# A recurrence stage whose interleaving is re-weighted: priorities for five streams, a tile-aware model, 64x64 tiles and a triangular inverse in one piece

## The chip, the core and the metric

The kernel runs on one core of a Trainium2 chip. The metric is the device time of one execution in microseconds (us). The engines are TensorE (PE), VectorE (DVE), ScalarE (ACT), GpSimd (POOL) and SyncE (SP, which issues most DMAs).

## The reference

One sequence of 512 tokens of width 1024 passes through an attention layer with an MLP, a recurrent layer with an MLP, and a second block with two further recurrences. All edits of code but those of the cost model are in the recurrent layer, RWKV-7, that runs in both directions over 16 heads of 64:

```python
xs = tuple(jnp.moveaxis(t, 1, 0) for t in (r, w, k, v, kk, a))
_, out = lax.scan(step, jnp.zeros((nB, H, N, N), F32), xs)
...
r = mix(0) @ w_r
k = mix(2) @ w_k
v = mix(3) @ w_v
...
for d in range(2):
    ...
    decay = jnp.exp(-jnp.exp(w_log.astype(F32)))
    a = jax.nn.sigmoid(a0[d] + (xa @ a1[d]) @ a2[d])
    g = jax.nn.sigmoid(xg @ g1[d]) @ g2[d]
    kd = heads(k * (1 + (a - 1) * k_a))
    ...
    o = rwkv7_scan(*ins)
    ...
    bonus = jnp.sum(rh * kd * r_k.astype(F32), axis=-1, keepdims=True) * vh
    dir_out.append((group_norm(o, gn_w, gn_b) + bonus.reshape(nB, S, D)) * g.astype(F32))
y = dir_out[0] + dir_out[1]
return y.astype(h.dtype) @ w_o
```

The step of the scan updates, for each head and direction, a 64x64 state that decays, forgets along `kk` and takes in `v` along `kd`; the output is the state read along `r`.

## The kernel before

**How the scan is tiled.** The scan is computed in chunks of 64 tokens, eight for each direction. Two heads make a pair p, and the pairs p = 0 to 7 follow one another. For each pair the work is cut into generator functions, the streams, in `rwkv` (from L1507):

- `values` (L1507): the projection `v`, with weights split into two parts (matmuls `mb<-mx,whi` and `mb<-mx,wlo`); it runs once over all columns.
- `front` and `half` for each direction d: the low-rank decays and gates (`mb<-lhl,wh`), a running sum on DVE, exponentials on ACT, and 16 products into tiles `ar` and `bk`, 128x256 each.
- `scores` (four iterations i): the chunk's products (`mb<-ar,bk`), two masks on DVE into `at`, stores of the diagonal blocks to DRAM (`nd`), transposes of `bk` (`mb<-ident,bk`).
- `inverse` (L1694): reads the diagonal blocks back into `X` and `XL` and inverts 128 unit triangles of 16x16 on DVE, by 28 small products and sums, then stores `X` to DRAM.
- `early`: loads `v`, spreads it over the tiles `uv` (`mb<-cmat,v`).
- `merge`: loads the inverses (`yd`), transposes them (`zd`) and builds the inverse of 64x64 from the small ones, by some 200 matmuls on 32x32 tiles of PE with copies between.
- `mid` (four iterations i, two chunks each): `ahead` (`mb<-ident,ar`, `mb<-uv,at`), `ax`, the product with the inverse (`mb<-ax,tt`), `ta`, and `mb<-at,ta`, whose result with `ar` and the identity becomes the transition `m`.
- `chain`: eight steps. Each one multiplies the state `ss` with `m` (`cp<-ss,m`), adds what the chunk brings (`cp<-uv,at`), and copies and scales the new state by four ACT copies, and the output `o` by two.
- `post`: the norm of the heads (two squares on ACT, two reduces into `rg` on DVE, a power on POOL, two multiplies `o<-o,rg` on DVE), transposes (`mb<-ident,o`), the bonus and the gate.

**What orders the work.** `Net.weave` (L36) takes the streams and interleaves them by a model: it asks each stream for its next piece, computes from `cost` (L48) and `wait` when that piece could start, and emits the one that starts first, less the stream's lead. On each engine the instructions then run in exactly the order of their emission, since `account` ties each to the one before it. Three stages are built this way: the attention, the scan, and the second block. A stream may also yield a condition: `chain(p)` waits until `post(p-1)` is done; `scores` are held at most nine tiles of `at` ahead of the chain; `mid` at most three transitions `m`; `early` starts with the chain of p-1; `inverse` waits for the four scores, `merge` for `inverse` and `early`. PSUM has five banks with the tag `mb` for all but the chain, which has three of its own.

For PE, `cost` tells tiles side by side apart by their column alone.

Of the kernel before, what the change touches and what calls it, by code (L numbers as in the profile page):

```python
# [10 lines left out]
F32 = mybir.dt.float32  # L11
# [13 lines left out]
class Net:  # L25
# [10 lines left out]
    def weave(self, streams, slow=1.0):  # L36
# [5 lines left out]
        seen = len(nc.cur_bb.bb.instructions)  # L42
        free, ready, last, used, cols, table = {}, {}, {}, [128], {}, [AF.Exp]

# [3 lines left out]
        def cost(i, e, t):  # L48
            n = math.prod(c for _, c in i.outs[0].ap[1:])
            if e == "PE":  # L50
                (_, col), (rows, m) = i.tile_position, i.tile_size
                if m == 128 or m != used[0] or col in used[1:]:
                    used[:] = [m]
                beside = len(used) > 1
                used.append(col)
                one = i.ins[0].dtype in (F32R, mybir.dt.bfloat16)
                passes = 2 if i.is_transpose else 1 if one else 4

                tick = int(t / 3.413)
                c = passes * (max(n, 64) if one or i.is_transpose else m / 2 if beside else max(n, m)) * 0.417e-3  # L60
                c *= slow if cols.get(tick - 1, 0) > 3060 else 2 * slow
                tick = int((t + c) / 3.413)
                cols[tick] = cols.get(tick, 0) + passes * n * rows / 128
                return c + 0.004
# [1226 lines left out]
    def rwkv(self, g_pre, mu_p, mu_n, w_r, w_k, w_v, w_o, k_k, k_a, r_k, gn_w, gn_b, w0, w1, w2, a0, a1, a2,  # L1291
# [35 lines left out]
        with ExitStack() as c0:  # L1327
# [110 lines left out]
            with ExitStack() as c1:  # L1438
# [4 lines left out]
                self.weights(cw, 2, 2)  # L1443
                vout = self.pool(cw, "vout")
                late = {}
# [11 lines left out]

                tts, ss, tas = zeros("tt", [8, 2, 64]), zeros("ss", [2, 128]), zeros("ta", [2, 2, 2, 64])
                for j, t in enumerate(tts + ss + tas):
                    (V, G)[j % 2].memset(t, 0.0)  # L1460
# [46 lines left out]
                def values():  # L1507
# [14 lines left out]
                    for j in range(KD):  # L1522
# [7 lines left out]
                        yield AC, b  # L1530
                        t = vout.tile([128, S], F32, name="vo", tag="vo")
                        ACT(t, b, AF.Copy)
# [161 lines left out]
                def inverse(p, st):  # L1694

                    yield lambda: done["pre"] > p
                    XL = sh.tile([128, 16, 32], F32, name="XL", tag="v1")
                    for q in range(2):
# [8 lines left out]
                    for j in range(1, 15):  # L1707
                        n = 15 - j
                        t = xt[:, :j * n].rearrange("p (i c) -> p i c", c=n)
                        TT(V, t, X[:, 0:j, j].unsqueeze(2).to_broadcast([128, j, n]),  # L1710
                           X[:, j, j + 1:16].unsqueeze(1).to_broadcast([128, j, n]), M)
                        yield DV, xt
                        TT(V, X[:, 0:j, j + 1:16], X[:, 0:j, j + 1:16], t, AD)
                        yield DV, X
                    V.memset(flat(X)[:, 0:512:33], 1.0)
# [3 lines left out]
                def early(p, st):  # L1719
# [7 lines left out]
                    st["uv"] = uv  # L1727
                    for d in range(2):
                        yield PO,
                        G.memset(uv[d][H(d)], 0.0)  # L1730
                    yield PE, v
# [79 lines left out]
                def mid(p, st):  # L1811
# [5 lines left out]
                    def ahead(i):  # L1817
                        b = bank().rearrange("p (j h e x) -> p j h e x", j=2, h=2, e=2)
                        at = st["q", i]
                        for j in range(2):  # L1820
# [3 lines left out]
                            for hp in range(2):  # L1824
                                for d in range(2):
                                    MM(b[H(d), j, hp, 1, :], at[:, j, hp, 2 * d, H(d)], uv[d][:, cs[d], hp, :], True, True)
                        return b

                    for i in range(4):
# [17 lines left out]
                        yield AC, b  # L1847
                        ta = tas[i % 2]
                        for d in range(2):
                            ACT(ta[H(d), d], b[H(d), :, :, 0:64], AF.Copy)  # L1850
                        yield AC, b
# [3 lines left out]
                        yield PE, ta  # L1855
                        b = bank().rearrange("p (j d x) -> p j d x", j=2, d=2)
                        for j in range(2):
                            for d in range(2):
                                for hp in range(2):
                                    MM(b[H(hp), j, d, :], ta[:, d, j, hp, :], lhs(at[:, j], d, hp), True, True)  # L1860
                        yield DV, b
                        m = mp.tile([128, 2, 2, 128], F32, name="m", tag="m", bufs=3)
                        for d in range(2):
                            cs = slice(6 - 2 * i, 8 - 2 * i) if d else slice(2 * i, 2 * i + 2)
                            r = ar[d][:, cs, 1 - d, :]
                            TT(V, m[:, :, d, H(d)], b[:, :, d, H(d)], r[:, ::-1] if d else r, AD)
                        i4 = lambda t: t.rearrange("p j d x -> p j (d x)")[:, :, 64:192].rearrange("p j (d x) -> p j d x", d=2)
                        TT(V, i4(m), i4(b), ident2.unsqueeze(1).unsqueeze(1).to_broadcast([128, 2, 2, 64]), AD)
                        st["m", i] = m
# [94 lines left out]
                def each(f):  # L1964
                    for p in range(8):
                        yield from f(p, sts[p])

                self.weave([(values(), 0.0)] + [(each(f), 0.0) for f in (
                    chain, mid, inverse, early, merge, scores, front, lambda p, st: half(p, st, 0), lambda p, st: half(p, st, 1), post)])


# [166 lines left out]
```

## Time and profile before

| | |
|---|---|
| median of 3 runs | 2333.58 us (2332.74 to 2334.99) |
| the profiled execution | 2329.99 us |
| its span | 2328.2 us |
| mean granted clock of TensorE | 0.952 |
| busy over the span: PE, DVE, ACT, POOL | 2135.0, 1276.4, 1077.6, 85.3 us |

The profiled execution is 3.6 us below the median. Busy time tells how long an engine had an instruction under way. A matmul in 32-bit floats shows as two records, so the counts of the trace are twice those of the code. The clock granted to PE is a share of 2.4 GHz.

### The profile page before, as it was taken

The page shows a single profiled execution, that of the slowest core. Times are in us where ns is not written, and L with a number is a line of the kernel's source. Part 1 is how long each engine was busy: PE and PEld are TensorE (multiplying, and loading weights), DVE is VectorE, ACT ScalarE, POOL GpSimd, SP SyncE. Part 2 cuts the span into 40 slices and gives each one's busy share as a digit, 9 for nine tenths or more (in the row PEclk, how much of TensorE's full clock was granted, in tenths as well). Part 3 has the DMA queues.
Part 4 walks back from the last instruction along what each step waited for, and adds up shares of the span by engine and source line. Part 5 has one row for each costly group of instructions (what it writes and reads, how often), then busy time and mean ns, then how long its engine had stood idle before and what let it go on. Part 6 is the DMA issues. An engine that isn't in the chain of part 4 may idle for free. (4 is left out here: it accounts for less than half of the span.)

```text
span 2328.2 us, 40334 instructions
## 1 busy us (share of the span) xinstructions
PE 2135.0 (92%) x16330; PEld 1719.8 (74%) x16330; DVE 1276.4 (55%) x2562; ACT 1077.6 (46%) x1950; POOL 85.3 (4%) x123
## 2 busy tenths in 40 slices
PE   7898999999968788888898689999999999999998
PEld 6777788888856666666676568887787877788877
DVE  4656542333388765667664255387645566633353
ACT  4555353342356554777766544333233444522232
POOL 0000000000000000011100100000000000000000
PEclk9999999999979987989999899999999988899999
DMA  5311233233224233222222343324334544233341
GB/s 173 104 55 54 71 110 92 90 100 100 91 71 121 91 99 80 61 61 57 52 55 46 105 133 109 91 90 144 111 111 142 143 126 119 54 95 90 107 145 55
DMA packets 321028, 221.52 MB, mean 95 GB/s; under 512 B 82414, under 2 KB 274442, under 8 KB 320842
## 3 DMA queue, kind: packets, MB, share of 16 engines
q1 hardware_dynamic: 319402, 213.70, 32.3%
q10 hardware_dynamic: 1440, 5.24, 0.7%
q8 instruction: 129, 2.11, 0.4%
q14 instruction: 57, 0.47, 0.1%
HBM read 187.62 MB, written 27.07 MB: 92 GB/s over the span
## 5 line engine op out<-in xcount | busy, mean ns | idle before, releaser
L160 ACT ACTIVATE whi<-raw 128x1024 fp32r<-128x1024 f32 x220 | 231.1, 1052 | 585.9 <-PE mm L223 297.3
L161 DVE TENSOR_TENSOR wlo<-raw,whi 128x1024 fp32r<-128x1024 f32 x220 | 266.5, 1214 | 368.0 <-ACT whi L160 365.4
L222 PE MATMUL mm<-uth,whi 128*128 128x512 f32 (+1 forms) x1088 | 412.9, 382 | 2.1 <-ACT uth L196 2.1
L223 PE MATMUL mm<-utl,whi 128*128 128x512 f32 (+1 forms) x1088 | 406.6, 374 | 5.5 <-DVE utl L197 5.5
L224 PE MATMUL mm<-uth,wlo 128*128 128x512 f32 (+1 forms) x1088 | 406.6, 374 | 0.0
L223 PEld LDWEIGHTS mm<-utl,whi 128*128 128x128 f32 x1088 | 209.0, 192 | 43.2 <-DVE utl L197 6.7
L222 PEld LDWEIGHTS mm<-uth,whi 128*128 128x128 f32 x1088 | 208.3, 192 | 41.0 <-ACT uth L196 3.5
L224 PEld LDWEIGHTS mm<-uth,wlo 128*128 128x128 f32 x1088 | 208.8, 192 | 37.3 <-issue 1.1
L224 PE MATMUL mm<-whi,hl 128*128 128x512 f32 x512 | 200.6, 394 | 0.0
L222 PE MATMUL mm<-whi,hh 128*128 128x512 f32 x512 | 200.5, 394 | 0.0
L223 PE MATMUL mm<-wlo,hh 128*128 128x512 f32 x512 | 199.9, 393 | 0.0
L224 PEld LDWEIGHTS mm<-whi,hl 128*128 128x128 f32 x512 | 96.3, 188 | 22.0 <-issue 0.2
L223 PEld LDWEIGHTS mm<-wlo,hh 128*128 128x128 f32 x512 | 96.3, 188 | 21.6
L222 PEld LDWEIGHTS mm<-whi,hh 128*128 128x128 f32 x512 | 96.3, 188 | 21.5 <-issue 0.4
L222 PE MATMUL mm<-whi,uth 128*128 128x512 f32 x224 | 88.6, 401 | 8.5 <-ACT whi L160 6.4
L224 PE MATMUL mm<-whi,utl 128*128 128x512 f32 x224 | 88.7, 399 | 0.0
L223 PE MATMUL mm<-wlo,uth 128*128 128x512 f32 x224 | 88.5, 398 | 0.0
L1301 ACT ACTIVATE ss<-cp,wc 64x64 f32<-64x64 f32 x224 | 69.1, 309 | 27.6 <-PE cp L1302 22.7
L282 DVE TENSOR_TENSOR acc<-mm,acc 128x512 f32<-128x512 f32 x48 | 33.0, 688 | 77.6 <-PE mm L224 77.6
L223 PE MATMUL mm<-mx,whi 128*128 128x512 f32 x160 | 66.0, 412 | 4.6 <-DVE mx L1289 4.4
L222 PE MATMUL mm<-mx,whi 128*128 128x512 f32 x160 | 62.1, 415 | 7.2 <-ACT mx L1288 6.0
L1299 DVE SCALAR_TENSOR_TENSOR mt<-u_pad,vcol,mt 128x512 f32<-128x512 f32 x96 | 66.8, 745 | 1.4 <-ACT mt L1301 1.3
(554 smaller groups left out, 3966.3 us busy)
## 6 DMA issues: line engine op xcount, KB each, us to landing
raw<-in_mlp_w_dram SPq DMA_DIRECT2D x128, 512.0 KB
raw<-in_w_in_dram SPq DMA_DIRECT2D x44, 512.0 KB
raw<-in_attn_w_in_dram SPq DMA_DIRECT2D x18, 512.0 KB
gbt<-in_norm_g_dram ACTq DMA_DIRECT2D x8, 512.0 KB
raw<-in_attn_w_out_dram SPq DMA_DIRECT2D x8, 512.0 KB
raw<-in_rk_w_k_dram SPq DMA_DIRECT2D x8, 512.0 KB
h_s<-h SPq DMA_DIRECT2D x8, 512.0 KB
raw<-in_rk_w_r_dram SPq DMA_DIRECT2D x8, 512.0 KB
```

The lines of the kernel that those rows point to most:

```text
L160: nc.scalar.activation(out=hi[:, :n], in_=raw[:, :n], func=AF.Copy)
L161: nc.vector.tensor_tensor(out=lo[:, :n], in0=raw[:, :n], in1=hi[:, :n].bitcast(F32), op=ALU.subtract)
L222: mm(out, lhsT=lhs[0], rhs=rhs[0], start=start, stop=False)
L223: mm(out, lhsT=lhs[0], rhs=rhs[1], start=False, stop=False)
L224: mm(out, lhsT=lhs[1], rhs=rhs[0], start=False, stop=stop)
L282: nc.vector.tensor_tensor(out=a, in0=p, in1=a, op=ALU.add)
L1299: STT = lambda e, o, a, s, b, o0, o1: e.scalar_tensor_tensor(out=o, in0=a, scalar=s, in1=b, op0=o0, op1=o1)
L1301: ACT = lambda o, i, f, **k: nc.scalar.activation(out=o, in_=i, func=f, **k)
```

## The change

The change has nine parts, all in one diff: (1) `cost` knows a tile by its rows, columns and place, and counts a small fixed time for a tile beside another one; (2) the pool `vout` goes, `values` use the buffers of `TQ()`; (3) the zeroed tiles `tas` go, `ta` is written by one ACT copy of 128x256 in place of two of 64x256; (4) `XL` has a buffer of its own; (5) `inverse` doesn't yield between its 28 products; (6) `early` doesn't zero halves of `uv`; (7) `ahead` multiplies 64 rows of `at` and `uv`; (8) `mid` multiplies `at` and `ta` by halves, on four 64x64 tiles, into two banks, and `m` is made by four sums of 128x128; (9) `chain` has a lead of 0.5, `mid`, `merge` and `inverse` of 0.4, `early` of 0.3.

```diff
         def cost(i, e, t):
             n = math.prod(c for _, c in i.outs[0].ap[1:])
             if e == "PE":
-                (_, col), (rows, m) = i.tile_position, i.tile_size
-                if m == 128 or m != used[0] or col in used[1:]:
-                    used[:] = [m]
+                at, (rows, m) = i.tile_position, i.tile_size
+                if (rows, m) != used[0] or at in used[1:]:
+                    used[:] = [(rows, m)]
                 beside = len(used) > 1
-                used.append(col)
+                used.append(at)
...
-                c = passes * (max(n, 64) if one or i.is_transpose else m / 2 if beside else max(n, m)) * 0.417e-3
+                c = passes * (max(n, 64) if one or i.is_transpose else 8 if beside else max(n, 64)) * 0.417e-3
...
-                        t = vout.tile([128, S], F32, name="vo", tag="vo")
+                        t = TQ()
...
-                    XL = sh.tile([128, 16, 32], F32, name="XL", tag="v1")
+                    XL = sh.tile([128, 16, 32], F32, name="XL", tag="XL")
...
                            X[:, j, j + 1:16].unsqueeze(1).to_broadcast([128, j, n]), M)
-                        yield DV, xt
                         TT(V, X[:, 0:j, j + 1:16], X[:, 0:j, j + 1:16], t, AD)
-                        yield DV, X
...
-                    for d in range(2):
-                        yield PO,
-                        G.memset(uv[d][H(d)], 0.0)
...
-                                    MM(b[H(d), j, hp, 1, :], at[:, j, hp, 2 * d, H(d)], uv[d][:, cs[d], hp, :], True, True)
+                                    MM(b[H(d), j, hp, 1, :], at[H(1 - d), j, hp, 2 * d, H(d)], uv[d][H(1 - d), cs[d], hp, :], True, True)
...
-                        ta = tas[i % 2]
-                        for d in range(2):
-                            ACT(ta[H(d), d], b[H(d), :, :, 0:64], AF.Copy)
+                        ta = mp.tile([128, 2, 2, 64], F32, name="ta", tag="ta")
+                        ACT(ta, b[:, :, :, 0:64], AF.Copy)
...
-                        b = bank().rearrange("p (j d x) -> p j d x", j=2, d=2)
+
+                        bs = [bank()[:, :256].rearrange("p (j x) -> p j x", j=2) for _ in range(2)]
                         for j in range(2):
-                            for d in range(2):
-                                for hp in range(2):
-                                    MM(b[H(hp), j, d, :], ta[:, d, j, hp, :], lhs(at[:, j], d, hp), True, True)
-                        yield DV, b
+                            for hp in range(2):
+                                for d in range(2):
+                                    MM(bs[d][H(hp), j, :], ta[H(d), j, hp, :], lhs(at[:, j], d, hp)[H(d)], True, True)
                         m = mp.tile([128, 2, 2, 128], F32, name="m", tag="m", bufs=3)
                         for d in range(2):
+                            yield DV, bs[d]
...
-                            TT(V, m[:, :, d, H(d)], b[:, :, d, H(d)], r[:, ::-1] if d else r, AD)
-                        i4 = lambda t: t.rearrange("p j d x -> p j (d x)")[:, :, 64:192].rearrange("p j (d x) -> p j d x", d=2)
-                        TT(V, i4(m), i4(b), ident2.unsqueeze(1).unsqueeze(1).to_broadcast([128, 2, 2, 64]), AD)
+                            TT(V, m[:, :, d, H(d)], bs[d][:, :, H(d)], r[:, ::-1] if d else r, AD)
+                            TT(V, m[:, :, d, H(1 - d)], bs[d][:, :, H(1 - d)], ident2.unsqueeze(1).to_broadcast([128, 2, 64]), AD)
...
-                self.weave([(values(), 0.0)] + [(each(f), 0.0) for f in (
+                lead = {chain: 0.5, mid: 0.4, merge: 0.4, inverse: 0.4, early: 0.3}
+                self.weave([(values(), 0.0)] + [(each(f), lead.get(f, 0.0)) for f in (
                     chain, mid, inverse, early, merge, scores, front, lambda p, st: half(p, st, 0), lambda p, st: half(p, st, 1), post)])
```

**How the order moves.** Three places, a row as the engine's order has it.

PE at the end of `values`, before: the last products of `values` (`mx,...`) are followed by the first stage of `merge(0)` (`zd,at` and `yd,at`).

```order
L222 MATMUL mb<-mx,whi 128x512
L223 MATMUL mb<-mx,whi 128x512
L224 MATMUL mb<-mx,wlo 128x512
L1302 MATMUL mb<-zd,at 32x32 x2
L1302 MATMUL mb<-yd,at 32x32 x2
```

And with the change: they are followed by `ahead(0)` of `mid(0)`.

```order
L222 MATMUL mb<-mx,whi 128x512
L223 MATMUL mb<-mx,whi 128x512
L224 MATMUL mb<-mx,wlo 128x512
L1302 MATMUL mb<-ident,ar_6222 64x2x64
L1302 MATMUL mb<-ident,ar_6227 64x2x64
L1302 MATMUL mb<-uv_6672,at 64x64
```

`merge(0)` now stands between earlier products of `values`.

DVE in `post(2)`, before: the first multiply `o<-o,rg` with what stands around it; `xt` and `X` are the inverse.

```order
L1298 TENSOR_TENSOR xt__9981<-X 128x44
L1298 TENSOR_TENSOR X<-X,xt__9981 128x4x11
L1298 TENSOR_TENSOR xt__9981<-X 128x50
L1298 TENSOR_TENSOR X<-X,xt__9981 128x5x10
L1298 TENSOR_TENSOR xt__9981<-X 128x54
L1298 TENSOR_TENSOR X<-X,xt__9981 128x6x9
L1298 TENSOR_TENSOR xt__9981<-X 128x56
L1298 TENSOR_TENSOR X<-X,xt__9981 128x7x8
L1298 TENSOR_TENSOR o<-o,rg 128x512
L1300 TENSOR_SCALAR rn<-mb 128x8
L1298 TENSOR_TENSOR xt__9981<-X 128x56
L1300 TENSOR_SCALAR tmp<-tmp 128x8x64
```

And with the change: the end of the inverse, which now lies whole between the power and the first multiply, then both multiplies; `tmp<-r,tmp` and `wl` are of `half` and `front`.

```order
L1298 TENSOR_TENSOR xt__10054<-X 128x26
L1298 TENSOR_TENSOR X<-X,xt__10054 128x13x2
L1298 TENSOR_TENSOR xt__10054<-X 128x14
L1298 TENSOR_TENSOR X<-X,xt__10054 128x14
L1712 MEMSET X 128x16
L1298 TENSOR_TENSOR tmp<-r,tmp 128x512
L1298 TENSOR_TENSOR wl<-w,wh 128x512
L1298 TENSOR_TENSOR o<-o,rg 128x512
L1298 TENSOR_TENSOR at<-mb,mk 128x2x2x128 x2
L1654 COPY bns<-mb 128x8 x2
L1299 SCALAR_TENSOR_TENSOR tmp<-mb,vcol_4919,tmp 128x256 x2
L1298 TENSOR_TENSOR o<-o,rg 128x512
```

From `post`'s first reduce to its second multiply there are now 73 instructions, and 34 before; the 16 products of `half` are among them.

PE in `chain(3)`, before: twelve rows between two of its steps (`cp<-...`), of `mid`, of `scores` (`ar,bk`, `ident,bk`).

```order
L1302 MATMUL mb<-ax,tt_6032 64x128 x8
L1302 MATMUL mb<-ar_9800,bk_9803 128x128 x2
L1302 MATMUL mb<-ar_9808,bk_9809 128x128 x2
L1302 MATMUL mb<-ar_9800,bk_9803 128x128 x2
L1302 MATMUL mb<-ar_9808,bk_9809 128x128 x2
L1302 MATMUL mb<-at,ta_6035 64x128 x8
L1687 MATMUL mb<-ident,bk_9803 128x128
L1687 MATMUL mb<-ident,bk_9809 128x128
L1687 MATMUL mb<-ident,bk_9803 128x128
L1687 MATMUL mb<-ident,bk_9809 128x128
L1302 LDWEIGHTS zb
L1302 MATMUL cp<-zb 128x256
```

And with the change: twelve rows after the fourth step. One product of `mid` and one of `post` (`lg`) lie between, and the scores stand behind the last steps or in the gap between two chains.

```order
L1302 MATMUL cp<-ss_6031,m 128x128 x2
L1302 MATMUL mb<-ax,tt_6029 64x128 x8
L1302 MATMUL mb<-lg_4941,wg 128x512
L1302 LDWEIGHTS zb
L1302 MATMUL cp<-zb 128x256
L1302 MATMUL cp<-uv_9199,at 64x64 x4
L1302 MATMUL cp<-uv_9200,at 64x64 x4
L1302 MATMUL cp<-ss_6030,m 128x128 x2
L1302 LDWEIGHTS zb
L1302 MATMUL cp<-zb 128x256
L1302 MATMUL cp<-uv_9199,at 64x64 x4
L1302 MATMUL cp<-uv_9200,at 64x64 x4
```

## Rows read from the trace of the kernel before

**Rows 1.** Busy time by stage: attention, scan, second block (columns in the first row).

```profile
core 0: us, PE busy (x) PEld busy (x) DVE busy (x) ACT busy (x) POOL busy (x), PEclk, DMA share, GB/s
...
57.00:236.00 179.00, 159.97 (x1090) 127.07 (x1088) 106.95 (x239) 100.32 (x224) 0.00 (x0) 0.98 0.23 70
...
910.00:1340.00 430.00, 365.51 (x7587) 285.51 (x7573) 250.41 (x695) 292.27 (x764) 44.73 (x38) 0.92 0.25 61
...
1800.00:2020.00 220.00, 211.19 (x1009) 167.88 (x1009) 141.65 (x219) 103.99 (x144) 0.60 (x6) 0.89 0.43 114
```

**Rows 2.** The same view between first and last state copies of each chain.

```profile
909.60:939.30 29.70, 25.37 (x661) 21.30 (x660) 15.97 (x38) 10.15 (x26) 0.23 (x2) 0.80 0.23 49
939.30:980.50 41.20, 35.63 (x793) 28.25 (x788) 23.56 (x69) 32.65 (x85) 2.70 (x3) 0.90 0.25 50
980.50:1002.00 21.50, 20.61 (x304) 15.58 (x303) 18.62 (x56) 17.22 (x35) 5.95 (x5) 0.84 0.21 54
1002.00:1033.90 31.90, 27.36 (x630) 21.93 (x628) 17.16 (x46) 22.35 (x66) 0.96 (x2) 0.95 0.28 63
1033.90:1060.00 26.10, 22.03 (x385) 16.60 (x384) 22.16 (x67) 20.49 (x44) 5.81 (x5) 0.93 0.20 50
1060.00:1086.90 26.90, 25.07 (x613) 19.64 (x612) 14.56 (x37) 20.19 (x60) 0.93 (x1) 1.00 0.34 75
1086.90:1113.20 26.30, 20.80 (x385) 15.46 (x384) 22.22 (x68) 20.52 (x44) 5.84 (x6) 1.00 0.18 47
1113.20:1140.70 27.50, 25.35 (x614) 19.77 (x612) 14.62 (x37) 20.24 (x60) 0.94 (x1) 1.00 0.29 65
1140.70:1166.80 26.10, 23.55 (x384) 18.30 (x384) 20.54 (x63) 19.98 (x42) 5.59 (x5) 0.80 0.18 47
1166.80:1194.80 28.00, 25.44 (x613) 19.89 (x614) 15.77 (x42) 20.25 (x61) 0.94 (x1) 1.00 0.25 52
1194.80:1215.50 20.70, 17.80 (x325) 13.79 (x325) 18.77 (x65) 11.40 (x28) 3.85 (x2) 0.92 0.22 50
1215.50:1244.40 28.90, 26.35 (x693) 21.25 (x693) 9.92 (x22) 21.10 (x64) 1.06 (x2) 1.00 0.27 55
1244.40:1262.90 18.50, 15.52 (x214) 12.75 (x213) 11.80 (x46) 11.23 (x27) 3.78 (x2) 0.91 0.13 35
1262.90:1290.90 28.00, 23.10 (x641) 18.49 (x641) 6.64 (x14) 19.26 (x58) 0.00 (x0) 0.94 0.22 47
1290.90:1306.20 15.30, 12.09 (x181) 9.42 (x178) 7.51 (x19) 8.09 (x21) 2.90 (x1) 1.00 0.01 2
1306.20:1323.30 17.10, 14.44 (x187) 10.47 (x187) 3.73 (x8) 15.01 (x48) 0.00 (x0) 1.00 0.40 136
```

**Rows 3.** PE's timeline: start us, us, instruction, output from inputs, tile, shape, records.

```profile
1157.80 1.09 PE L1302 MATMUL mb<-at,ta 128*64 128x128 f32 x16
1158.83 0.50 PE L1302 MATMUL mb<-lhl,wh 128*128 128x512 f32 x1
...
1160.19 0.40 PE L1302 MATMUL mb<-uv,at 128*64 128x64 f32 x8
1160.42 0.39 PE L1302 MATMUL mb<-ident,ar 128*64 128x128 f32 x4
1160.64 0.40 PE L1302 MATMUL mb<-uv,at 128*64 128x64 f32 x8
1160.97 0.66 PE L1504 MATMUL mb<-ident,tmp 128*128 128x128 f32 x4
```

**Rows 4.** PE's timeline: the first matmuls of ahead(0).

```profile
925.54 0.70 PE L1302 MATMUL mb<-ident,ar 128*64 128x128 f32 x4
```

**Rows 5.** Groups of DVE instructions in 910 to 1340: busy us, mean ns, idle before.

```profile
L1298 DVE TENSOR_TENSOR bk<-tmp 128x256 f32<-128x256 f32 x48 | 20.1, 418 | 0.7 <-PE mb L1687 0.7
...
L1298 DVE TENSOR_TENSOR m<-mb,ar 128x128 f32<-128x128 f32 x64 | 15.4, 281 | 25.0 <-PE mb L1302 24.4
...
L1298 DVE TENSOR_TENSOR m<-mb,ident 128x256 f32<-128x256 f32 x32 | 13.2, 414 | 0.0
```

**Rows 6.** DVE's timeline: one product of the inverse.

```profile
1099.74 0.20 DVE L1298 TENSOR_TENSOR X<-X,xt__9981 128x36 f32<-128x36 f32 x1
```

More of the change, by code (lines that the diff above doesn't have):

```diff
@@ L42, in weave @@
         seen = len(nc.cur_bb.bb.instructions)
-        free, ready, last, used, cols, table = {}, {}, {}, [128], {}, [AF.Exp]
+        free, ready, last, used, cols, table = {}, {}, {}, [None], {}, [AF.Exp]
         def wait(by, e):
@@ L1443, in rwkv @@
                 self.weights(cw, 2, 2)
-                vout = self.pool(cw, "vout")
                 late = {}
@@ L1456, in rwkv @@
                 zeros = lambda nm, shape: [sh.tile([128] + shape, F32, name=f"{nm}{j}") for j in range(2)]
-                tts, ss, tas = zeros("tt", [8, 2, 64]), zeros("ss", [2, 128]), zeros("ta", [2, 2, 2, 64])
-                for j, t in enumerate(tts + ss + tas):
+                tts, ss = zeros("tt", [8, 2, 64]), zeros("ss", [2, 128])
+                for j, t in enumerate(tts + ss):
                     (V, G)[j % 2].memset(t, 0.0)
```

## The prediction

> **What bounds the kernel now.** I read the stages first. The edited program is interleaved in three places, and in two of them little can be won: in the attention stretch PE is busy 159.97 of 179.00 us, in the second block's 211.19 of 220.00 [rows 1]. Those orders are only reshuffled there; I give them 0, with ±4 for both. The recurrence stretch is different: 430 us, PE busy 365.51, ACT 292.27, DVE 250.41 [rows 1]. No engine is full, so an order with its waits sets the time.
>
> Then I cut that stretch at the state copies of `chain`, eight steps for each of the eight head pairs p [rows 2]. A **phase** is one pair's chain; a **gap** lies between two of them, since `chain(p+1)` starts only when `post(p)` is done. Phases take 41.2, 31.9, 26.9, 27.5, 28.0, 28.9, 28.0 and 17.1 us, gaps 21.5, 26.1, 26.3, 26.1, 20.7, 18.5 and 15.3; together 384.0. Two things are to be seen. The last phase has the same eight steps but nothing else to carry, and takes 17.1 us; in the others PE is busy over 25 of some 27 us with other streams' matmuls. So a phase is as long as the foreign PE work in it, down to a floor of about 17. A gap is a path: squares on ACT, two reduces on DVE, the power on POOL, two multiplies on DVE, transposes on PE; in it PE is busy 20.8 and DVE 22.2 of 26.3 us, so what DVE or PE has queued ahead of a step of `post` lengthens it.
>
> **The change, part by part.**
>
> *Order on PE.* From the two orders I counted the matmuls between the chains' first and last. I price eight of N = 128 at 1.03 us (the eight of `at,ta`, 16 records, from 1157.80 to 1158.83) [rows 3], also the scores and 128-wide transposes, whose sizes are the nearest; an N = 512 one at four times one of these, some 0.4.
>
> - Start: `merge(0)` now precedes the last products of `values`, and the first thing after them is `mid(0)`. Before, 29.7 us passed from 909.6 to the first state copy [rows 2], the last 13.8 of them from the first matmuls of `ahead(0)` on, which start at 925.54 [rows 4]. Without the rest: **−15.9**.
> - Phase 0: 196 merge matmuls, eight of `half`, eight scores, eight transposes and other small ones leave it, 12.3 us by the prices, 14 at the granted clock of 0.90 [rows 2]: **−14**. Phase 1 keeps as much as it had: 0. Phase 2 gives up 16 `at,ta` (2.1), 8 `ax,tt` (1.0), 24 scores (3.1), 12 transposes (1.5) and 12 of `ahead` (0.5), 8.2 in all, and takes four of `half`: **−7**. Phases 3 to 6 likewise **−7.5, −8, −6.3, −5**; the last one 0. Sum of phases −47.8.
> - Gaps: what left the phases stands there. In gap 2, 24 more scores, 12 more transposes, 8 more `ax,tt`, 8 more broadcasts, four of `half`: +8.8 us of PE. By the same counts +11.5, +1.7, +9.8, +2.7, +2.6 and +2.3 in gaps 0, 1, 3, 4, 5, 6. Taken fully, for PE was near its fill there: gap 0 **+12**, gap 3 **+9.8**, the last three together **+7.9**.
>
> *Order on DVE.* In gaps 1 and 2 the orders show 73 instructions from `post`'s first reduce to its second multiply, where 34 stood. Of the 39 more, 16 are products of `half` of 418 ns (6.7 us) [rows 5]; about 8 are masks or products of twice that size beyond those that left, at some 0.7 (an estimate from 418 ns for the half; 5.6 us); 11 are of the inverse at 0.20 [rows 6] (2.2); with copies some +15 us. The engine runs in order, so the multiply that waited for POOL alone now stands behind the inverse block and the whole of `half`. Bounds for gap 1: +2, if this fills time that DVE idled, and +15, if all of it is added; I take **+10**. For gap 2, where PE's +8.8 comes on top: +9 and +24; I take **+14**, as the two run beside each other. Gaps in all +53.7.
>
> *The block of 28 DVE products.* Before, they lay spread among other work, now they are one piece of some 5.6 us (28 at 0.20). That brings `merge(p)` forward, which the chain does not wait for (its gate is `post`); apart from the order above: 0.
>
> *Four tiles.* `at,ta` went through two tiles side by side, now four: 1.03 becomes about 0.57, on 32 iterations −14.9 us of PE; that is in the counts above, where each now counts half. The prices leave out changes of tile size. Eight `uv,at` take 0.23 us to the next start if the size stays (1160.19 to 1160.42) and 0.33 if it changes (1160.64 to 1160.97) [rows 3], so 0.10 each; the order has 433 of them where 374 were, +5.9 us, of which half lies on the path: **+3**. The four adds into `m` of 281 ns replace two of 281 and one of 414 [rows 5], +0.15 us on each of 32: `mid` runs up to three iterations ahead of the chain, so 0; uncovered +4.7.
>
> The trace says DVE waits there for PE, 24.4 us in sum [rows 5], so shorter matmuls reach `m` sooner. The Trainium skill, "TensorEngine Tiling (Array Packing)", PSUM Bottleneck, speaks against that: after tiling makes TensorE faster, the copies out of PSUM may become the limit. By that rule the 14.9 us would not come back, since DVE has more to do per `m`; half of it on the path would put the sum 7 us higher (a rival below).
>
> *Small ones.* 32 ACT copies fewer and 16 POOL memsets fewer: ACT is idle a third of the stretch and POOL nine tenths [rows 1]; 0. The larger `tmp` buffers' use by `values` and an own buffer for `XL`: 0.
>
> **Sum.** −15.9 − 47.8 + 53.7 + 3 = −7.0. The profiled execution took 2329.99 (span 2328.2), so 2323.0; it lies 3.6 under the median 2333.58, which gives **2326.6, say 2327**. The change mostly moves work from phases to gaps, and the answer is a small difference of large terms. Their ends: phases all at the floor, DVE terms at the low ends: −31; only half of the phases' gain and gaps 1 and 2 at their high ends: about +31. A measurement of this kernel tells about 0.2% (4.7 us) from no change.
>
> **Rivals.**
>
> A, *slower*: the gaps stretch fully. In gaps 1 and 2 `post`'s multiplies stand behind the loads of `XL`, the block and `half`, and the chain, the longest path, waits for them: +15 and +24 where I had +10 and +14 (+15), while phases 2 to 6, that hold a merge with its copies and transposes between chain steps, shorten by a tenth less than priced (+4): 2346. It decides if the first multiply starts more than about 12 us after its power has ended. For it: the order on DVE is fixed and shows it. Against it: DVE idles some 4 us of 26 in gaps, 12 of 27 in phases [rows 2].
>
> B, *clearly faster*: phases fall to the floor. The last phase shows 17.1 us; with foreign PE work of under 5 us left in phases 2 to 6, each could take 18 to 19 in place of my 20 to 23 (−13), and gaps 0 and 3 could hide half of their added PE work beside `post`'s path (−10): 2304. Against it: merge matmuls in a phase wait for copies in order.
>
> C, *nothing measurable*: the four tiles give nothing, by the rule on copies, or the earlier start of chain 0 is lost while the first gap waits for its many scores: 2333. PE's low granted clock from 802 on (0.80 in the start row [rows 2]) speaks for part of it.
>
> **How the numbers follow.** The forecast (2318 to 2334 by itself) has a chance of 0.38: faster 0.20, the same 0.13, slower 0.05. A 0.27: slower 0.24, the same 0.03. B 0.25, faster. C 0.10: the same 0.05, slower 0.04, faster 0.01. Together faster 0.46, the same 0.21, slower 0.33. The range reaches from B, 2303, past A to 2352, and leaves out the two ends.
>
> **What would show it.** Right: first state copy near 923 in place of 939.3; phase 0 under 30; phases 2 to 6 at 18 to 23; gaps 0 to 3 at 33 to 41; `at,ta` in about 0.6 us; less ACT and POOL work. Wrong: phases that stay at 27 (then foreign PE work did not set them), gaps 1 and 2 over 45 (A), or gaps 0 and 3 near 25 (B). A difference outside 910 to 1340 would show that the other two interleavings matter, which I priced at nothing.

## The result, and the profile after

The changed kernel takes 2418.65 us (median of 4 runs, 2417.38 to 2425.05), the kernel before 2334.28 (4 runs, 2332.74 to 2336.56): the ratio is 1.0366, 95% interval 1.0352 to 1.0380. It is 84 us slower, outside the predicted range. A few executions that took at least 6% longer than the rest (8042.08 us in one run below) are left out of all medians and ratios.

The profiled execution took 2425.05 us, 6.4 over its median, with a span of 2423.3 where the one before had 2328.2 (that execution lies 4.3 under its median, so the spans differ by 95.1 us and the medians by 84). The same view between the first and last state copies as in [rows 2] (the start, then phases and gaps in turn; of the rows left out, phases 4 to 6 are 18.2, 21.0 and 20.6 us long and gaps 4 to 6 39.7, 31.3 and 24.8):

```profile
927.40:933.10 5.70, 5.70 (x112) 4.44 (x111) 1.32 (x5) 2.48 (x7) 0.00 (x0) 1.00 0.12 46
933.10:955.20 22.10, 19.91 (x323) 15.48 (x321) 7.48 (x25) 17.21 (x55) 0.00 (x0) 1.00 0.05 9
955.20:1011.10 55.90, 40.80 (x830) 31.57 (x826) 49.03 (x145) 25.82 (x54) 5.79 (x6) 0.77 0.34 77
1011.10:1046.30 35.20, 32.51 (x663) 24.69 (x663) 9.37 (x22) 21.91 (x63) 0.00 (x0) 0.79 0.13 28
1046.30:1097.20 50.90, 34.28 (x457) 26.53 (x448) 27.81 (x88) 19.23 (x44) 4.76 (x4) 0.57 0.13 29
1097.20:1116.30 19.10, 18.40 (x511) 13.71 (x511) 5.19 (x10) 16.61 (x50) 0.00 (x0) 0.98 0.34 79
1116.30:1164.90 48.60, 33.69 (x504) 26.23 (x505) 35.22 (x100) 25.89 (x55) 10.30 (x4) 0.79 0.21 49
1164.90:1186.90 22.00, 19.82 (x586) 14.53 (x582) 7.31 (x13) 20.93 (x57) 0.00 (x0) 1.00 0.20 46
1186.90:1243.10 56.20, 36.57 (x739) 28.08 (x739) 34.84 (x99) 25.20 (x54) 6.39 (x5) 0.73 0.18 41
...
1398.70:1415.40 16.70, 15.44 (x185) 10.94 (x184) 3.76 (x8) 14.06 (x45) 0.00 (x0) 0.91 0.24 90
```

| part of the span, us | before | after | difference | predicted |
|---|---|---|---|---|
| up to the first state copy | 939.3 | 933.1 | -6.2 | -15.9 |
| the eight phases | 229.5 | 174.9 | -54.6 | -47.8 |
| the seven gaps | 154.5 | 307.4 | **+152.9** | +53.7 |
| from the last state copy on | 1004.9 | 1007.9 | +3.0 | 0 |

The 95.1 us of the span are all here. The forecast's +3 for changes of tile size was given to no part, so its column adds up to -10.0 and not to its -7.0. The phases fell, as forecast, all but phase 1 to about 17 to 22. The gaps doubled, and each of the seven is longer. In gaps 1 to 3 PE is busy 34 to 37 of 49 to 56 us and DVE 28 to 35, so no engine is full. The longest groups of waits of the changed kernel from 910 to 1435, POOL's and PE's loads left out (engine and line, what it waited for, us in total, times, longest):

```profile
DVE m L1298 <- PE mb L1302: 76.8, 24, 7.7
...
ACT uv L1301 <- PE mb L1302: 58.7, 5, 20.2
ACT ss L1301 <- PE cp L1302: 53.1, 24, 12.4
PE mb L1941 <- DVE o L1298: 38.1, 12, 9.6
```

Before, the first of these came to 24.4 [rows 5], and the others, in the same view from 910 to 1340, to 5.2, 22.7 and 9.8. DVE and ACT wait for PE and PE for DVE: a circle. The last row is `post`: its transposes on PE (L1941, before L1948) wait for its multiplies `o` on DVE.

**Gap 3 row by row.** Phase 3 ends at 1186.9, chain 4 starts at 1243.13. DVE's timeline of the changed kernel (start us, us, instruction, output from inputs; in brackets the idle time before it and what ended it):

```profile
1194.52 0.28 DVE L1298 TENSOR_TENSOR m<-mb,ident 128x128 f32<-128x128 f32 x1
...
1215.64 0.38 DVE L1703 COPY X<-XL 64x256 f32<-64x256 f32 x1
...
1222.53 0.67 DVE L1930 TENSOR_REDUCE rg<-tmp 128x8 f32<-128x512 f32 x1
...
1223.12 1.28 DVE L1298 TENSOR_TENSOR at<-mb,mk 128x512 f32<-128x512 f32 x2
...
1227.85 0.69 DVE L1930 TENSOR_REDUCE rg<-tmp 128x8 f32<-128x512 f32 x1 [3.31 <-ACT tmp L1301]
...
1235.04 0.68 DVE L1298 TENSOR_TENSOR o<-o,rg 128x512 f32<-128x512 f32 x1
```

and of PE and of ACT:

```profile
1223.85 0.58 PE L1302 MATMUL mb<-cmat,v 128*128 128x128 f32 x1 [8.09 <-DVE at L1298]
```

```profile
1198.02 0.38 ACT L1301 ACTIVATE ta<-mb 128x256 f32<-128x256 f32 x1 [3.04 <-PE mb L1302]
...
1203.71 0.38 ACT L1301 ACTIVATE ta<-mb 128x256 f32<-128x256 f32 x1 [3.48 <-PE mb L1302]
...
1205.31 0.61 ACT L1301 ACTIVATE tmp<-o 128x512 f32<-128x512 f32 x1
...
1225.96 1.20 ACT L1301 ACTIVATE uv<-mb 64x512 f32<-64x512 f32 x2 [18.50 <-PE mb L1302]
1227.18 0.63 ACT L1301 ACTIVATE tmp<-o 128x512 f32<-128x512 f32 x1
```

The first transition `m` for chain 4 is there at 1194.8, 7.9 us after phase 3. What chain 4 waits for is `post(3)`. Its first square ends on ACT only at 1205.92, 19.0 us after phase 3, where the gaps of the kernel before have 3.4 to 4.1. Three iterations of `mid` for chain 4 now stand ahead of it: their copies `ax`, `ta` and `uv` are twelve of the 23 ACT instructions between the last copy of `o` and the square, and ACT waits over 3 us for PE twice. In gaps 1 to 6 of the changed kernel the square ends 12.1 to 19.0 us after the phase. And the reduce that takes it runs at 1222.53, behind `half` and the whole inverse block (1215.64 to 1222.63). A mask `at` stands behind the block too, so a bank is held; PE idles 8.09 us, ACT behind it 18.50, and only then does the second square come, then the rest of `post`. The delay of one stretch of DVE work (`half`, then the block) went once round three engines. For comparison, ACT's timeline of the kernel before at the same square (phase 3 ends there at 1140.70):

```profile
1139.39 1.31 ACT L1301 ACTIVATE ss<-cp,wc 64x64 f32<-64x64 f32 x4
...
1143.47 0.63 ACT L1301 ACTIVATE tmp<-o 128x512 f32<-128x512 f32 x1
```

**Two gates.** Two ways end at a chain's start: `post` of the pair before, whose second multiply `o<-o,rg` I take as its mark, and scores, stores, inverse, `merge` and `mid` of its own pair, whose mark is the first `m`. (The first step itself takes `uv`, which the same iteration of `mid` writes just ahead of `m`.) Ends in us after the end of the last state copy of the chain before, chain start last:

| kernel, gap | post's second multiply | first m | next chain |
|---|---|---|---|
| before, 2 | 20.1 | 17.1 | 26.3 |
| after, 0 | 24.2 | **54.4** | 55.9 |
| after, 3 | **48.8** | 7.9 | 56.2 |

In gaps 1 to 6 of the changed kernel the second multiply ends at 45.7, 44.7, 48.8, 35.7, 28.9 and 22.4, the first `m` at 5 to 13. In gap 0 it is the other gate: the scores of pair 1 had been moved out of phase 0, their last mask ends at 959.15, and from there to the chain's start it takes 51.9 us. DVE's timeline there:

```profile
957.86 1.29 DVE L1298 TENSOR_TENSOR at<-mb,mk 128x512 f32<-128x512 f32 x2 [0.88 <-PE mb L1302]
...
967.32 0.44 DVE L1703 COPY X<-XL 64x256 f32<-64x256 f32 x1
...
983.82 0.71 DVE L1745 STREAM_TRANSPOSE zd<-yd 128x512 f32<-128x512 f32 x1 [0.69 <-issue]
...
1008.75 0.29 DVE L1298 TENSOR_TENSOR m<-mb,ar 128x128 f32<-128x128 f32 x1 [1.77 <-PE mb L1302]
```

From the mask through DRAM to `X` 8.2 us, from there with the block and DRAM again to `zd` 16.5, with `merge` and `mid` to `m` 24.9, then 2.4. In the kernel before, the way from a pair's last mask to its chain takes 65 to 82 us, but it begins before the phase ahead of the gap does.

### The profile page after: what moved, and what is told of

The parts are those of the page before. It is cut to its first block, busy times and chain, and to the rows that moved or that the text cites. A ratio compares the mean times of both kernels' runs of the same rounds, so it can differ in the third digit from the quotient of the medians.

```text
span 2423.3 us, 40317 instructions
## 1 busy us (share of the span) xinstructions
PE 2164.5 (89%) x16330; PEld 1729.6 (71%) x16330; DVE 1284.2 (53%) x2593; ACT 1064.2 (44%) x1918; POOL 75.3 (3%) x106
## 5 line engine op out<-in xcount | busy, mean ns | idle before, releaser
L223 PEld LDWEIGHTS mm<-wlo,hh 128*128 128x128 f32 x512 | 96.3, 188 | 21.7
```

Source lines behind the costliest of these rows:

```text
L223: mm(out, lhsT=lhs[0], rhs=rhs[1], start=False, stop=False)
```

## The experiments

All times are medians beside runs of the kernel before on the same chip; ratios with 95% intervals; sums of phases and gaps from each run's profiled execution (before: 229.5 and 154.5). *Buffers* stands for parts 2 and 4 of the change alone:

```diff
-                        t = vout.tile([128, S], F32, name="vo", tag="vo")
+                        t = TQ()
...
-                    XL = sh.tile([128, 16, 32], F32, name="XL", tag="v1")
+                    XL = sh.tile([128, 16, 32], F32, name="XL", tag="XL")
```

### Which part costs

**No leads** (the change, part 9 undone):

```diff
-                lead = {chain: 0.5, mid: 0.4, merge: 0.4, inverse: 0.4, early: 0.3}
+                lead = {}
```

> The change with all leads at 0; tiles, buffers, block and model stay. If the leads cost the 84 us (they put mid, merge and the inverse into the gaps between two chains, where post waits for them): 2310 to 2350 us, phases back to some 27 us and gaps to 20 to 28. If the model that takes tiles beside others for nearly free does it: still over 2390. If the inverse in one piece does it, since all 28 products stay between post's reduces and its second multiply: 2380 to 2420.

Measured: 2379.86, 1.0188 (1.0158 to 1.0219); phases 243, gaps 186. Over half of the loss stays without the leads.

**No leads and the old cost model** (parts 1 and 9 undone; the lines of `cost` as before).

> The change without leads and with the cost model of before; tiles, buffers and block stay. Leads theory: as the run without leads, 2310 to 2350. Model theory: 2320 to 2340, and at least 40 us below the run that has the new model and no leads. Block theory: 2380 to 2420.

Measured: 2376.31, 1.0192 (1.0146 to 1.0237); phases 222, gaps 198. The two intervals lie over each other: the model costs nothing that can be told.

**Tiles alone** (the same, and the 28 yields of the inverse back; parts 2 to 4 and 6 to 8 remain):

```diff
+                        yield DV, xt
                         TT(V, X[:, 0:j, j + 1:16], X[:, 0:j, j + 1:16], t, AD)
+                        yield DV, X
```

> The change with neither leads nor new model, and with the inverse's products yielding one by one: the four tiles, the 64-row products of ahead, one ACT copy for ta, no memsets, and the buffers. By all theories within 15 us of before; by the prediction's terms for the tiles 2326 to 2334 (PE 14.9 us less, half of it on the path); if the copies out of PSUM take the gain, 2334 to 2340.

Measured: 2335.39, 1.0007 (0.9986 to 1.0029). The tiles neither give nor take. The step from here to the run before it is the block: 41 us.

**Leads alone** (before, buffers, part 9).

```diff
+                lead = {chain: 0.5, mid: 0.4, merge: 0.4, inverse: 0.4, early: 0.3}
+                self.weave([(values(), 0.0)] + [(each(f), lead.get(f, 0.0)) for f in (
```

> The kernel before with the leads and the two buffers that they need (XL of its own, no vout); no new model, tiles or yields. Leads theory: 2390 to 2430, phases near 20 us, gaps 30 to 55. Model theory: 2330 to 2345, as before. Block theory: the lead of the inverse packs its products into one piece here too, so 2380 to 2420; it is told apart by the runs without leads.

Measured: 2370.74, 1.0150 (1.0119 to 1.0181); phases 179, gaps 261. This is outside all that was expected. The inverse's lead of 0.4 brings its 28 products close together here too (6.6 to 10.1 us from the first to the last, 7.5 to 21.3 before), so this run isn't free of the block. `post`'s first square is late here as in the changed kernel: in gaps 1 to 6 it ends 5.8 to 23.0 us after the phase, and 2.3 to 3.8 us in the runs without leads.

**Block alone** (before, buffers, part 5: the two yields between the products away).

> The kernel before with the inverse in one piece (and XL of its own, no vout): nothing else. If the block lengthens post's path by its own length of some 5.6 us in six or seven gaps: +34 to +42, 2368 to 2378, with gaps of 30 to 34 us and phases as before. If it hurts only together with the other parts: 2330 to 2345.

Measured: 2377.61 (three executions), 1.0191 (1.0125 to 1.0257); phases 244, gaps 192. The block by itself costs some 46 us (29 to 60 by the interval), as much as the change without leads. DVE's timeline of this run in gap 2, and the state copies on ACT around it:

```profile
1111.49 0.41 DVE L1298 TENSOR_TENSOR m<-mb,ident 128x256 f32<-128x256 f32 x1
...
1121.12 0.69 DVE L1934 TENSOR_REDUCE rg<-tmp 128x8 f32<-128x512 f32 x1
...
1129.55 0.15 DVE L1300 TENSOR_SCALAR rg<-rg 128x16 f32<-128x16 f32 x1
...
1136.09 0.68 DVE L1298 TENSOR_TENSOR o<-o,rg 128x512 f32<-128x512 f32 x1
```

```profile
1109.71 1.31 ACT L1301 ACTIVATE ss<-cp,wc 64x64 f32<-64x64 f32 x4
...
1142.67 1.31 ACT L1301 ACTIVATE ss<-cp,wc 64x64 f32<-64x64 f32 x4 [4.31 <-PE cp L1302]
```

`m` ends 0.9 us after the last state copy, so `post` alone decides. The small step on `rg` that feeds POOL's power needs the second reduce, which ends at 1121.81, but starts at 1129.55: the 28 products, 6.5 us, lie between. In the kernel before it starts in this gap at 1098.69, right behind the reduce that ends at 1098.62. This wait is 6.5 to 7.7 us in gaps 0, 2, 3 and 4 of the run; in gaps 1 and 5, too, all 28 products stand between the first reduce and the second multiply.

**Leads without the inverse's** (before, buffers; part 9 less `inverse: 0.4`).

> The kernel before with leads for chain, mid, merge and early, none for the inverse, whose products still yield one by one (XL of its own, no vout). If the leads cost by themselves, because scores and half then stand in the gaps: 2350 to 2375, phases near 20 us, gaps of 30 to 45. If all of it came through the inverse that the lead packs into one piece: 2325 to 2345.

Measured: 2360.00, 1.0123 (1.0063 to 1.0183); phases 187, gaps 253. With the inverse spread, leads for the others cost 28 us by themselves (15 to 43 by the interval), and gap 0 is 79.0: the round trip.

Taken in this order, 41 (block) + 4 (model, not told from 0) + 39 (the five leads, from the first run to the change) make up the 84. The shares depend on the order: leads alone, with the products close together, cost 36 us, so in that order the other 48 come only when tiles, model and the strict block meet the leads. The change with the old model or the old tiles, but with its leads, was not run; which of them brings the 48 stays open.

### Where the block stands

**Block in thirds** (block alone, with two yields back):

```diff
+                        if j in (5, 10):
+                            yield DV, X
```

> The kernel before with the inverse in three pieces in place of one or 28 (XL of its own, no vout). All of its products still stand between post's reduces and its second multiply. If that place is what costs: 2365 to 2385, as in one piece. If it is the length of the piece: about a third of the loss, 2340 to 2352.

Measured: 2365.38, 1.0136 (1.0104 to 1.0167); phases 243, gaps 183. The interval overlaps that of the whole block, so cheaper than whole is not shown, and it is far from free: in gaps 1 to 5 the order still has all 28 products between `post`'s first reduce and second multiply.

**Block held back by 2 and by 8** (block alone, with a negative lead):

```diff
+                lead = {inverse: -2.0}
```

> The kernel before with the inverse in one piece and a lead of -2 for it, so that it stands behind post's steps (XL of its own, no vout). If the block's place in post's path is what costs: 2320 to 2345, gaps 20 to 27. If the inverse is now late for merge and mid of the next pair, the gap waits for the round trip from scores to mid, over 50 us: 2360 to 2420. If one piece costs wherever it is: 2365 to 2385.

Measured: 2444.76, 1.0473 (1.0443 to 1.0503); phases 191, gaps 307.

> The same with a lead of -8. If place is the cause: 2315 to 2345, the phases longer and the gaps shorter than with -2. If the round trip decides, later still: 2370 to 2440. If one piece costs wherever it is: 2365 to 2385.

Measured (with -8.0): 2459.65, 1.0536 (1.0509 to 1.0562); phases 232, gaps 250.

The block left the path of `post`, and both runs are far slower, beyond all that was expected. The gaps alternate: with -2.0, gaps 1, 3 and 5 are 21.7, 21.8 and 14.4, shorter than before, and gaps 0, 2 and 4 are 73.6, 74.8 and 68.6. Gap 0 with -2.0, DVE's timeline (the last state copy ends at 971.58, the next chain's first starts at 1045.22):

```profile
985.60 0.68 DVE L1298 TENSOR_TENSOR o<-o,rg 128x512 f32<-128x512 f32 x1
...
998.13 0.38 DVE L1703 COPY X<-XL 64x256 f32<-64x256 f32 x1
...
1042.89 0.42 DVE L1298 TENSOR_TENSOR m<-mb,ident 128x256 f32<-128x256 f32 x1
```

`post` is done at +14.7, sooner than in the kernel before. But the block starts at +26.5, `m` comes at +71.7, the chain at +73.6: the second way is now the late one.

**The same with the tiles** (no leads, old model, and -4.0 or -8.0 for the inverse).

> The change without its leads and its model, with a lead of -4 for the inverse: tiles, buffers and block. Place: 2305 to 2340, against 2376 without the negative lead. Round trip: 2360 to 2430. One piece: 2365 to 2385.

> The same as the last with -8. Place: 2300 to 2340, as less PE work stands in the gaps. Round trip: 2370 to 2440. One piece: 2365 to 2385.

Measured: 2482.98, 1.0639 (1.0615 to 1.0662), and 2493.35, 1.0675 (1.0638 to 1.0712); in the first, phases 200, gaps 298. As above, and again above all that was expected.

**Block held back by 1**, without and with the tiles.

```diff
+                lead = {inverse: -1.0}
```

> The kernel before with the inverse in one piece and a lead of -1 for it (XL of its own, no vout): the block stands right behind post's second multiply for three pairs, between its steps for three. If its place in post's path is the cost: about half of 41 us comes back, 2340 to 2362, and in the gaps whose post is free of it the second multiply ends by +20 us in place of +26. If one piece costs wherever it is: 2370 to 2385. If already this makes the round trip from scores to mid the gate: over 2390.

Measured: 2351.42, 1.0076 (1.0053 to 1.0099); phases 218, gaps 194.

> The change without its leads and its model, and with a lead of -1 for the inverse: right behind post's second multiply for four pairs. Place: 2320 to 2355. One piece: 2365 to 2380. Round trip: over 2390.

Measured: 2354.31, 1.0089 (1.0058 to 1.0119); phases 232, gaps 178.

This takes back some 27 of the block's 46 us (without the tiles). Gap 1 without the tiles, where no product lies in `post`'s path, DVE's timeline (state copies end at 1044.11 and begin again at 1067.41):

```profile
1050.53 0.69 DVE L1934 TENSOR_REDUCE rg<-tmp 128x8 f32<-128x512 f32 x1 [0.62 <-ACT tmp L1301]
1051.25 0.17 DVE L1300 TENSOR_SCALAR rg<-rg 128x16 f32<-128x16 f32 x1
...
1059.43 0.68 DVE L1298 TENSOR_TENSOR o<-o,rg 128x512 f32<-128x512 f32 x1
```

From the reduce to `rg` 0.03 us in place of 7.7, `post` done at +16.0, the chain at +23.3 (26.1 before [rows 2]). Gaps 0 and 2 are 40.2 and 42.2: there `m` comes at +40.5 and +37.8. A place for the whole block that serves both gates in all gaps wasn't found.

### Moving post forward

**A lead for post alone** (before, buffers):

```diff
+                lead = {post: 0.5}
```

> The kernel before with a lead of 0.5 for post alone (XL of its own, no vout). If the gap is post's path and what DVE and PE have queued ahead of its steps, a post that goes first shortens each gap by 3 to 8 us: 2285 to 2320. If the gap is the latency of post's own steps, or the rest only moves: 2328 to 2345.

Measured: 2348.90, 1.0075 (1.0052 to 1.0098); phases 232, gaps 186. This is slower than either expectation. `post`'s second multiply comes at +11 to +16, where it had been at 13 to 22. Gaps 1 and 3 are shorter for it (21.7 and 23.6); the other five are longer, and in gaps 2, 4 and 6 it is the first `m` that comes late, at +30, +33 and +27, with the chain's start (29.6, 32.5 and 26.9).

**The change with a lead for post.**

```diff
-                lead = {chain: 0.5, mid: 0.4, merge: 0.4, inverse: 0.4, early: 0.3}
+                lead = {post: 0.5, chain: 0.5, mid: 0.4, merge: 0.4, inverse: 0.4, early: 0.3}
```

> The change with a lead of 0.5 for post too, as the chain has. In its order post's multiplies stand behind 0 to 5 products of half and, but for one pair, none of the inverse. If post's path through DVE makes gaps 1 to 6: they fall to 22 to 32 us, while gap 0, which waits for the round trip from scores to mid, stays over 45; 2335 to 2375. If something else makes them: 2400 to 2425.

Measured: 2388.28, 1.0230 (1.0203 to 1.0258); phases 206, gaps 236. It takes back 29 of the change's 84 us, and lies between the two expectations. `post`'s first square ends 1.8 to 3.0 us after the phase in all gaps, and its second multiply at +11 to +14. Gap 1 of this run, DVE (ACT's state copies end at 1044.70 and begin again at 1074.08):

```profile
1018.99 0.68 DVE L1298 TENSOR_TENSOR at<-mb,mk 128x512 f32<-128x512 f32 x1
...
1031.40 0.38 DVE L1703 COPY X<-XL 64x256 f32<-64x256 f32 x1
...
1055.21 0.68 DVE L1298 TENSOR_TENSOR o<-o,rg 128x512 f32<-128x512 f32 x1
...
1072.33 0.29 DVE L1298 TENSOR_TENSOR m<-mb,ar 128x128 f32<-128x128 f32 x1 [1.14 <-PE mb L1302]
```

From the end of the pair's last mask, 1019.67, to the chain it is 54.4 us, and over all gaps 45 to 61. With `post` out of the way the first `m` comes last in six of the seven gaps, within 1 us of the chain's start. In gap 3 the chain starts 11 us after the first `m`; DVE runs the whole inverse of a later pair in between (1199.13 to 1205.67).

**Other sets of leads.** The change with `lead = {post: 0.5, mid: 0.5, merge: 0.5}`:

> The change with leads of 0.5 for post, mid and merge alone. By the two gates of a gap (post; scores, inverse, merge and mid of the next pair) both go first and the chain's phase carries the rest: phases 28 to 36, gaps 15 to 24, 2310 to 2350. If the inverse in one piece costs wherever it stands: 2365 to 2385.

Measured: 2433.67, 1.0415 (1.0379 to 1.0452); phases 305, gaps 180. And the tiles alone with `lead = {post: 0.3, merge: 0.3}`:

> The run with the tiles alone, with leads of 0.3 for post and merge. By the two gates: gaps fall from some 28 to 15 to 22 us, phases grow from 27 to 30 to 36 us by the matmuls that move into them; 2300 to 2335. If the phases grow by all that the gaps lose: 2335 to 2360.

Measured: 2394.18, 1.0254 (1.0227 to 1.0282); phases 269, gaps 187. Both put foreign work back into the phases; neither is near the kernel before, and both are slower than was expected.

**A model with slow transfers** (before, buffers; `cost` takes 6 us for each DMA, to make it start round trips early):

```diff
+                cst = 6.0 if dma else
```

> The kernel before with 6.0 us in place of 2.2 for a transfer in the interleaving's model (XL of its own, no vout), near the 7 to 13 us that the trace shows from the last mask to the copy of XL. If wrong times of transfers are what makes the orders bad: 2290 to 2325. If not, within 10 us of before, or slower, as all three stages are reshuffled: 2325 to 2360.

Measured: 2555.83, 1.0947 (1.0894 to 1.0999); phases 207, gaps 304. It is some 195 us above the highest expectation: it orders all three stages anew, the part behind the last chain takes some 95 us more, and it says nothing of the two gates.

No version beat the kernel before. The block alone with a lead for `post`, and the change with the inverse spread, weren't run.

## Why the prediction was wrong

- **Phases**: -47.8 predicted, -54.6 measured. Right in the mechanism (foreign PE work sets their length) and nearly in size. By pairs it was off by a few us each way: phase 0 fell by 19.1 where 14 was forecast, and phase 1, forecast unchanged, grew by 3.3.
- **Four tiles**: `at,ta` went from 1.03 us to 0.62, the group from 39.9 to 24.5 us of PE, as worked out (0.57 and -14.9). PE's timeline of the changed kernel:

```profile
1193.14 0.67 PE L1302 MATMUL mb<-at,ta 64*64 64x128 f32 x16
1193.76 0.48 PE L1302 MATMUL mb<-ar,bk 64*128 64x128 f32 x2
```

  Half of it was to be on the path; the tiles alone gave nothing within 0.3%. That is the time which the rule on copies had: the Trainium skill, "TensorEngine Tiling (Array Packing)", PSUM Bottleneck. Its mechanism was not seen, though: in the run with the tiles alone (its profiled execution lies 11 us above its median) DVE still waited 22.2 us for PE ahead of `m`, against 24.4 before [rows 5], and ACT 50.8 us ahead of `ta`, against 29.3, so these copies waited for PE more than before, not less. Why the 15 us were lost there wasn't followed further.
- **Start**: -6.2 in place of -15.9. `merge(0)` did go ahead, and from the end of `values` to the first state copy 5.7 us remain of 29.7; but `values` ended at 927.4 instead of 909.6. Moving the work ahead was counted, that it takes its time there was not.
- **The block, "0 apart from order"**: this step failed. By itself it costs 46 us. The prediction saw that the block stands between the power and the first multiply and priced its instructions there at 2.2 us in two gaps, as 11 products beyond those that had been there; in the run with the block alone 6.5 us of products lie between two steps of `post` (7.7 us with the masks ahead of them), and all 28 lie between its first reduce and second multiply in six of seven.
- **Gaps**, +53.7, with +15 more at the high end of its two DVE terms: measured +152.9. This is the term that sank the sum. It added up the work that moved in, engine by engine, took DVE's and PE's as beside each other, and charged DVE in gaps 1 and 2 alone, and there only from the first reduce on. The trace shows the opposite: the engines wait in a circle, so one block delays all three, as gap 3 shows row by row. What stands ahead of `post`'s first square and first reduce, `mid` of the next pair above all, was put at nothing: in gaps 1 to 6 the first reduce starts 12.7 to 35.6 us after the phase, where 4.1 to 6.6 us had passed before. That is 87 us of the 118 by which these six gaps grew. Gap 0 was priced by its PE work (+12); it grew 34.4, because its gate was the round trip of 51.9 us from the scores that had left phase 0. The prediction called `post` the chain's gate and did not ask how late the other may come; its rival C named the first gap's many scores, but only as the loss of the earlier start.
- **Rival A** had the mechanism, `post`'s multiplies behind loads, block and `half`, and its sign: slower. Its price was 2346. It kept gaps 1 and 2 at 41 and 50, where 50.9 and 48.6 were measured, and gave the other gaps no more than the forecast did; gaps 0, 3, 4 and 5 grew by 34, 30, 19 and 13. Its sign came (gaps 1 and 2 over 45), but the condition that was to decide it did not: the first multiply starts at most 7.4 us after its power has ended, not 12, for the wait lies ahead of the power, at the square and at the reduces.
- **The small ones at 0** (buffers, copies, memsets) and the other two stages hold: tiles alone with all of the small ones are at 1.0007, and from the last state copy on it is 3 us more. The model, without leads, costs nothing that can be told; with leads it was not undone by itself.
- **Slips in its sums** change nothing of this. Half of the phases' gain and the two gaps at their high ends are +39 (23.9 and 15), not about +31; the end at 2366 is still far below 2419. Gaps 4 to 6 add up to 7.6, not 7.9. Four times a matmul at 1.03/8 is 0.5, not 0.4. The eight `uv,at` of its tile-size price are eight records, so four matmuls.

So two causes are shown: the block in `post`'s path (block alone, and what comes back with the block close behind `post`), and leads that clear the phases and put `mid`, scores and `half` into the gaps, ahead of steps of `post` (the leads without the inverse's, and the change with a lead for `post`). What each is worth within the 84 us is not shown, for they don't simply add up, and the part of the model and the tiles together with the leads is untested. How much of the phases' growth in the block's own run (244 for 229.5) belongs to it stays open.

## What to carry to other kernels

Where two long ways meet at each turn of a loop, price a new order by the end of each way, not by the work that was moved: write down when either gate opens and how much slack the other has. A short path over many engines must not have a long piece ahead of any step on any engine's queue; here, making 28 small instructions one piece took no instruction away and cost 46 us. Count from the path's first step: most of the growth of gaps 1 to 6 lay ahead of the first reduce, where the count of the prediction began. And priority for the longest chain only pays if what feeds its next turn still starts early enough.

## What was not expected of the hardware

PE's granted clock fell in the gaps: 0.57 to 0.79 in the mean of a gap, where the gaps before had 0.80 to 1.00 [rows 2]. Inside gap 3 of the changed kernel, by stretches:

```profile
1195.00:1203.00 8.00, 7.97 (x120) 5.77 (x119) 5.67 (x12) 2.17 (x6) 0.00 (x0) 1.00 0.12 22
1203.00:1210.00 7.00, 2.58 (x34) 1.68 (x32) 4.60 (x15) 2.83 (x7) 0.00 (x0) 0.80 0.26 70
1210.00:1216.00 6.00, 3.18 (x80) 2.66 (x79) 5.87 (x17) 0.00 (x0) 0.23 (x2) 0.50 0.17 44
...
1237.00:1243.10 6.10, 6.03 (x193) 4.32 (x189) 2.07 (x5) 1.66 (x3) 1.64 (x1) 0.64 0.08 15
1243.10:1250.00 6.90, 6.90 (x125) 5.23 (x125) 4.57 (x8) 6.51 (x20) 0.00 (x0) 1.00 0.22 35
```

At the full level, 2.4 GHz, PE is busy throughout up to 1203; then it waits for more than half of 7 us, and from 1210 the row shows 0.50, 1.2 GHz. The mean is still 0.64 in the 6.10 us just ahead of the chain, where PE is busy for 6.03, mostly with a merge. So a wait in a gap is paid twice: the matmuls behind it, which are on the way to the next chain, run at the lower level (four records of `post`'s transposes take 1.11 us at 1240.39, and 0.63 in the kernel before at 1162.89). How much of the 153 us this is wasn't measured by itself.
